# Receptance, second low-rank and gate weights split ahead into DRAM, partly beside the first stage

## The chip, the cores and the metric

One core of a Trainium2 chip runs the whole program. The metric is the device time of one execution in microseconds (us); the median of the runs stands for a kernel.

## The reference

Two residual layers over 512 tokens of width 1024, each followed by a gated convolutional FFN. Layer 0 mixes tokens with a chunked spatial gate, layer 1 is RWKV-7. All of it is float32.

```python
# layer 0
z = gelu(h @ w_in + b_in);  u, v = split(z);  v = rms_norm(v, g_v)
v = einsum(causal w_s, v in blocks of 128) + b_s
h = h + (u * v) @ w_out
# layer 1
xx = token_shift(h) - h;  xr, xw, xk, xv, xa, xg = (h + xx * mu[i] for i in range(6))
r = xr @ w_r;  k = xk @ w_k;  v = xv @ w_v
w = -softplus(-(w0 + tanh(xw @ w1) @ w2)) - 0.5
a = sigmoid(a0 + (xa @ a1) @ a2)
g = sigmoid(xg @ g1) @ g2
y = wkv7_scan(r, exp(-exp(w)), k, v, -kk, kk * a)      # a 64x64 state per head, 16 heads
h = h + (group_norm(y) * ln_w + ln_b + bonus) * g @ w_o
# after each layer
h = h + (silu(gate) * val) @ w_down,  gate, val = split(conv3(rms_norm(h) @ w_up) + conv_b)
```

## The kernel before

Activations lie transposed in SBUF, eight tiles `h[k]` of 128 features by 512 tokens. A float32 product is made of three matmuls in the faster 32-bit format (`mm3`, lines 295 to 297): a number x is split into a high part, ScalarE's cast of x (line 213, tiles named `wh`, `mxh` and so on), and a low part, x minus the high part, a subtraction on VectorE (line 214, `wl`, `mxl`; GpSimd does some of the activations' ones). The parts' products high·high, low·high and high·low add up in PSUM.

The stages follow each other on the one core: the spatial gate (`sgu`), the first FFN (`ffn`, 22 steps of two up-projections, then eight down-projections), RWKV, the second FFN, the final norm. In RWKV, `rwkv_first` makes the first low-rank products and the receptances r, and `rwkv_main` weaves three things: the chunk products and the scan, the inversion of small triangular blocks, and a filler of dense projections (keys, values, gates, output).

Weights come in tiles of 128 by 1024. `weights()` (line 229) loads a tile raw into one of two buffers `w32` and splits it, in halves of 512 columns, into `wh` and `wl`, four buffers of each. A raw tile is so loaded up to two tiles ahead, and the casts run up to four halves ahead of TensorE; a cast waits until TensorE is done with the buffer that it writes.

For keys, values, output and the first gate weights (`wk`, `wv`, `wo`, `g1`) the splitting has been done earlier. `make_parts()` (line 242) is a generator; each step loads one piece of 128 by 512 (`pw`, two buffers), casts it to `pwh`, subtracts to `pwl` (one buffer each) and stores both to DRAM (`wkd`, `wvd`, `wod`, `g1d`), all DMAs on SP's queue. The first FFN takes two steps of it per up-projection step for the first 15 of them, one for the rest, and two per down-projection. `parts()` (line 261) then loads the ready parts straight into `wh` and `wl`.

The receptances still use `weights()`. `wra` holds the first 512 output features as four tiles, each with two k: TensorE runs k = 0 to 7, four outputs each, three matmuls each, 96 in all; between, each k's operand is scaled (line 673), mixed (`mix`, lines 623 and 624) and split. `wrb` holds the other 512 as four tiles of one output each, taken in two pairs; in a pair TensorE goes over k and gives each of the two tiles three matmuls per k. The second low-rank factors (`second_factors`, lines 726 to 731) are loaded raw by SP four times, two pairs of features each, cast by ScalarE and subtracted by VectorE. The second gate weights (`gate_weights`, line 1063) are loaded on ScalarE's queue, 128 rows and 32 rows, the latter stacked (`stack`, line 219): high, high and low part in three groups of 32 rows.

What sets the order: each engine executes its instructions in the order written down by the framework's scheduler, which places an instruction of low priority where its model finds the engine free; `issue_after` ties a step behind the last instruction of an engine. DMAs stand in the queue of the engine that issues them (ScalarE or SP), and a DMA that waits for a buffer holds back everything behind it on that engine.

## Time and profile before

| | us |
|---|---|
| median of the 3 runs (1298.95, 1301.09, 1313.26) | 1301.09 |
| the profiled execution | 1305.46 |
| its span, first to last instruction | 1303.7 |
| TensorE busy / idle in the span | 1262.6 / 41.1 |
| VectorE, ScalarE, GpSimd busy | 852.5, 627.9, 129.9 |
| spatial gate, about | 0 to 155 |
| first FFN, about | 155 to 524 |
| `rwkv_first`, about | 524 to 582 |
| products and scan, about | 582 to 905 |
| second FFN and final norm, about | 905 to 1304 |

Rows of the profile name engines as PE (TensorE matmuls), PEld (TensorE weight loads), DVE (VectorE), ACT (ScalarE), POOL (GpSimd) and SP; ACTq and SPq are the issuing of DMAs in ScalarE's and SP's queues. L213 is line 213 of the kernel before. In a timeline a row is start, duration, engine, line, operation, output and inputs; in brackets the engine's idle time before it and what ended that. A matmul's shown length overlaps the next one's start, so its pace is read from start to start.

### The profile page before, as it was taken

The page shows a single profiled execution, that of the slowest core. Times are in us where ns is not written, and L with a number is a line of the kernel's source. Part 1 is how long each engine was busy: PE and PEld are TensorE (multiplying, and loading weights), DVE is VectorE, ACT ScalarE, POOL GpSimd, SP SyncE. Part 2 cuts the span into 40 slices and gives each one's busy share as a digit, 9 for nine tenths or more (in the row PEclk, how much of TensorE's full clock was granted, in tenths as well). Part 3 has the DMA queues.
Part 4 walks back from the last instruction along what each step waited for, and adds up shares of the span by engine and source line. Part 5 has one row for each costly group of instructions (what it writes and reads, how often), then busy time and mean ns, then how long its engine had stood idle before and what let it go on. Part 6 is the DMA issues. An engine that isn't in the chain of part 4 may idle for free.

```text
span 1303.7 us, 19609 instructions
## 1 busy us (share of the span) xinstructions
PE 1262.6 (97%) x7578; PEld 1015.2 (78%) x7578; DVE 852.5 (65%) x1379; ACT 627.9 (48%) x1072; POOL 129.9 (10%) x140
## 2 busy tenths in 40 slices
PE   8999999999999999999999988999999999999996
PEld 6878888888888888777777766767888888888886
DVE  5565478888875444756889686754677777772223
ACT  5544455555554333565776636512544444442221
POOL 3100100000000001210121011321200000000001
PEclk9999999999999999999999899999999999999998
DMA  7332458777557664336888697795233233333332
GB/s 254 96 102 83 130 177 249 246 247 241 172 170 218 202 214 154 89 112 164 242 225 264 171 239 177 179 223 156 82 99 98 97 97 98 97 95 102 89 89 77
DMA packets 110924, 205.84 MB, mean 158 GB/s; under 512 B 18224, under 2 KB 50224, under 8 KB 110832
## 3 DMA queue, kind: packets, MB, share of 16 engines
q10 hardware_dynamic: 39024, 113.66, 29.1%
q1 hardware_dynamic: 71808, 90.95, 24.0%
q8 instruction: 59, 0.97, 0.3%
q14 instruction: 33, 0.27, 0.1%
HBM read 155.02 MB, written 49.55 MB: 157 GB/s over the span
## 4 chain that ended last, share of the span: by engine, by line
PE 78%; DVE 8%; issue 3%; DMA 3%; ACT 2%; POOL 1%; SPq 0%; ACTq 0%; DVEq 0%; POOLq 0%
PE mm L295 8%; PE mm L297 8%; PE mm L296 8%; PE aux L295 6%; PE aux L296 6%; PE aux L297 6%; PE us L297 5%; PE us L295 5%; PE us L296 5%; PE e L297 5%; PE e L296 5%; PE e L295 5%; DVE pr L973 1%; DVE tt L974 1%; DVE lq L900 1%
## 5 line engine op out<-in xcount | busy, mean ns | idle before, releaser
L213 ACT CAST wh<-w 128x512 fp32r<-128x512 f32 x340 | 206.3, 610 | 344.9 <-PE mm L296 87.7
L214 DVE TENSOR_TENSOR wl<-w,wh 128x512 fp32r<-128x512 f32 x340 | 232.0, 684 | 179.7 <-ACT wh L213 178.2
L295 PE MATMUL mm<-mxh,wh 128*128 128x512 f32 (+1 forms) x384 | 156.9, 409 | 0.0
L297 PE MATMUL mm<-mxh,wl 128*128 128x512 f32 (+1 forms) x384 | 153.2, 399 | 0.3 <-DVE wl L214 0.3
L296 PE MATMUL mm<-mxl,wh 128*128 128x512 f32 (+1 forms) x384 | 152.1, 396 | 0.0
L322 POOL TENSOR_TENSOR ss<-ss,sq 128x512 f32<-128x512 f32 x30 | 40.9, 1364 | 783.9 <-issue 594.9
L519 ACT ACTIVATE cv<-z,par 128x512 f32<-128x512 f32 x88 | 71.7, 817 | 42.3 <-DVE z L517 42.2
L295 PEld LDWEIGHTS mm<-mxh,wh 128*128 128x128 f32 (+1 forms) x384 | 72.4, 188 | 18.0 <-issue 2.6
L297 PEld LDWEIGHTS mm<-mxh,wl 128*128 128x128 f32 (+1 forms) x384 | 72.4, 189 | 17.6 <-DVE wl L214 0.8
L295 PE MATMUL e<-mxh,wh 128*128 128x512 f32 x216 | 84.5, 391 | 0.0
L296 PEld LDWEIGHTS mm<-mxl,wh 128*128 128x128 f32 (+1 forms) x384 | 72.5, 189 | 15.4 <-issue 0.7
L296 PE MATMUL e<-mxl,wh 128*128 128x512 f32 x216 | 84.1, 389 | 0.0
L297 PE MATMUL e<-mxh,wl 128*128 128x512 f32 x216 | 84.1, 389 | 0.0
L296 PE MATMUL aux<-mxl,wh 128*128 128x512 f32 x208 | 81.4, 391 | 2.7 <-POOL mxl L214 2.0
L295 PE MATMUL aux<-mxh,wh 128*128 128x512 f32 x208 | 81.5, 392 | 0.3 <-ACT mxh L213 0.3
L295 PE MATMUL us<-mxh,wh 128*128 128x512 f32 x208 | 81.2, 391 | 0.0
L520 DVE SCALAR_TENSOR_TENSOR cv<-z,par,cv 128x512 f32<-128x512 f32 x88 | 66.1, 751 | 22.9 <-ACT cv L519 22.6
L297 PE MATMUL aux<-mxh,wl 128*128 128x512 f32 x208 | 81.0, 390 | 0.0
L297 PE MATMUL us<-mxh,wl 128*128 128x512 f32 x208 | 81.0, 389 | 0.0
L296 PE MATMUL us<-mxl,wh 128*128 128x512 f32 x208 | 80.9, 389 | 0.0
L521 DVE SCALAR_TENSOR_TENSOR cv<-z,par,cv 128x512 f32<-128x512 f32 x88 | 66.0, 752 | 2.9
L296 PEld LDWEIGHTS aux<-mxl,wh 128*128 128x128 f32 x208 | 39.1, 188 | 12.3 <-POOL mxl L214 2.7
(1091 smaller groups left out, 2700.3 us busy)
## 6 DMA issues: line engine op xcount, KB each, us to landing
w<-in_wup ACTq DMA_DIRECT2D x88, 512.0 KB, 3.7
w<-in_wdn ACTq DMA_DIRECT2D x32, 512.0 KB, 3.6
st<-std SPq DMA_DIRECT2D x30, 384.0 KB, 5.8
std<-lq SPq DMA_DIRECT2D x32, 256.0 KB, 4.4
w<-in_wdn ACTq DMA_DIRECT2D x16, 384.0 KB, 3.4
w<-in_wsu ACTq DMA_DIRECT2D x8, 512.0 KB, 3.6
w<-in_wso ACTq DMA_DIRECT2D x8, 512.0 KB, 3.6
pw<-in_wk SPq DMA_DIRECT2D x16, 256.0 KB, 3.8
```

The source lines that it names most:

```text
L213: nc.scalar.copy(hi[r, :n], src)
L214: (lo_eng or nc.vector).tensor_tensor(lo[r, :n], src, hi[r, :n].bitcast(F32), ALU.subtract)
L295: mm(acc, wh, xh, start=first, stop=False)
L296: mm(acc, wh, xl, start=False, stop=False)
L297: mm(acc, wl, xh, start=False, stop=last)
L322: nc.gpsimd.tensor_tensor(self.ss, self.ss, self.sq, ALU.add)
L519: nc.scalar.activation(c, z[:, 2:], AF.Identity, scale=cw(2, i), bias=self.p("conv_b", l * 44 + i))
L520: nc.vector.scalar_tensor_tensor(c, z[:, 1:T + 1], cw(1, i), c, ALU.mult, ALU.add)
L521: nc.vector.scalar_tensor_tensor(c, z[:, 0:T], cw(0, i), c, ALU.mult, ALU.add)
L900: V.tensor_tensor(lq[:, :, 1 - hd], qs[hd], masks.unsqueeze(1).to_broadcast([P, U, P]), ALU.mult)
L973: V.tensor_tensor(q, a, b, ALU.mult)
L974: V.tensor_tensor(tt[:, 0:nj, j + 1:32], tt[:, 0:nj, j + 1:32], q, ALU.add)
```

## The change

`make_parts` takes a list of pieces. The list (`part_list`) now also holds `wra` and `wrb` (16 pieces), the second low-rank factors `l2` (4) and the second gate weights `g2` (4): 75 pieces instead of 51. The first 21 (all of `wra` and `wrb`, five of `wk`) are made in the spatial gate: six beside its v products, ten beside u and the gating, six beside its output, with one step to drain. The other 54 are made in the first FFN, which takes two steps per up-projection step for 17 instead of 15 of them. The receptances load their parts with `parts()` on ScalarE's queue, eight halves of two DMAs for `wra` and as many for `wrb`; the second factors come as three DMAs on SP's queue instead of two, with no cast and no subtraction; the gate weights come on SP's queue instead of ScalarE's, without cast, subtraction or stacking.

```diff
@@ part_list and make_parts
+        for n, ds in self.wd.items():                  # wra, wrb, wk, wv, wo
+            for m, d in enumerate(ds):
+                for c in (slice(0, 512), slice(512, 1024)):
+                    at.append((A[n][m][:, c], [(j, rows, d[:, j, c]) for j in range(2)]))
...
-                    src, _, c = at[i]
-                    w.append(pool.tile([P, 512], F32, tag="pw", bufs=2, name=self.uid("pw"))[:, 0:c.stop - c.start])
-                    nc.sync.dma_start(w[i], src[:, c])
+                    src = at[i][0]
+                    r, n = src.shape
+                    w.append(pool.tile([P, 512], F32, tag="pw", bufs=2, name=self.uid("pw"))[0:r, 0:n])
+                    nc.sync.dma_start(w[i], src)
                 if i:
...
+                    if r == 32:
+                        x = [None, None, pool.tile([P, 512], F32R, tag="pwh", bufs=1, name=self.uid("pws"))]
+                        self.stack(x[2], w[i - 1], False)
+                    else:
+                        x = self.split(pool, w[i - 1], [P, 512], "pw", bufs=1)
+                    for j, rows, dst in at[i - 1][1]:
+                        nc.sync.dma_start(dst, x[j][rows, 0:n].bitcast(F32))
@@ sgu
+            parts = self.make_parts(sp, self.part_list()[:SGU_PARTS])
                     w = self.weights(A["wsv"][hf, kk], cut=hf == kk == 0)
+                    for _ in range((0, 0, 1, 1, 1, 1, 1, 1)[4 * hf + kk]):
+                        next(parts, None)
...
                 w = self.weights(A["wsu"][m])
+                if m < KT - 1:
+                    next(parts, None)
...
                 y.append(self.split(sp, t, [P, T], f"y{m}"))
+                if m % 2 == 0 and m < 6:
+                    next(parts, None)
...
                 w = self.weights(A["wso"][m])
+                if 0 < m < KT - 1:
+                    next(parts, None)
@@ ffn
-            parts = self.make_parts(fp) if self.next == "rwkv" else iter(())
+            parts = self.make_parts(fp, self.part_list()[SGU_PARTS:]) if self.next == "rwkv" else iter(())
-                for _ in range(2 if j < 15 else 1):
+                for _ in range(2 if j < 17 else 1):
@@ rwkv_first
-            w = self.weights(A["wra"][kk])
+            w = self.parts("wra", kk, False)
-            ws = [self.weights(A["wrb"][m + j]) for j in range(2)]
+            ws = [self.parts("wrb", m + j, False) for j in range(2)]
@@ second_factors
-            for j in range(2):
-                w = w32[:, 512 * j:512 * j + 2 * P]
-                nc.sync.dma_start(w, A["l2"][j][:, P * p:P * p + 2 * P])
-                S.copy(l2[j], w)
-                V.tensor_tensor(l2[2][H[j]], w[H[j]], l2[j][H[j]].bitcast(F32), ALU.subtract)
+            for i, t in enumerate(l2):
+                nc.sync.dma_start(t.bitcast(F32), self.l2d[:, i, P * p:P * p + 2 * P])
@@ gate_weights
-            self.wq.dma_start(w32[:, 0:512], A["g2"][0:P, cols])
-            self.wq.dma_start(w32[0:32, 512:], A["g2"][P:P + 32, cols])
-            ws = ep.tile([P, 512], F32R, tag="gw", bufs=1, name=self.uid("gw"))
-            self.stack(ws, w32[0:32, 512:], False)
-            return (*self.split(ep, w32[:, 0:512], [P, 512], "gw", bufs=1), ws)
+            t = [ep.tile([P, 512], F32R, tag=f"gw{i}", bufs=(2, 2, 1)[i], name=self.uid("gw")) for i in range(3)]
+            for i, n in enumerate((P, P, 96)):
+                nc.sync.dma_start(t[i][0:n].bitcast(F32), self.g2d[g][0:n, i])
+            return t
```

The order of the instructions moves with it, at three places above all (line numbers of the change differ from those of the kernel before; a tile's name is followed by running numbers).

First, VectorE at the start of the receptances, from the first scaling of h to the low part of the first operand `mxl` (`mt` is a mixed operand, `lt` and `lu` the scaled low-rank products). Before:

```order
L673 SCALAR_TENSOR_TENSOR h0_66<-h0_66,par_65,rb_917_4597 128x512
L673 SCALAR_TENSOR_TENSOR h1_67<-h1_67,par_65,rb_917_4597 128x512
L214 TENSOR_TENSOR wl_935_4676<-w32_933_4673,wh_934_4675 128x512
L624 SCALAR_TENSOR_TENSOR mt_927_4633<-h0_66,omu_4458,mt_927_4633 128x512
L624 SCALAR_TENSOR_TENSOR mt_930_4654<-h1_67,omu_4458,mt_930_4654 128x512
L673 SCALAR_TENSOR_TENSOR h2_68<-h2_68,par_65,rb_917_4597 128x512
L214 TENSOR_TENSOR mxl_929_4637<-mt_927_4633,mxh_928_4636 128x512
```

and in the change:

```order
L711 SCALAR_TENSOR_TENSOR h1_67<-h1_67,par_65,rb_987_4798 128x512
L711 SCALAR_TENSOR_TENSOR h2_68<-h2_68,par_65,rb_987_4798 128x512
L711 SCALAR_TENSOR_TENSOR h3_69<-h3_69,par_65,rb_987_4798 128x512
L662 SCALAR_TENSOR_TENSOR mt_996_4832<-h0_66,omu_4659,mt_996_4832 128x512
L662 SCALAR_TENSOR_TENSOR mt_999_4853<-h1_67,omu_4659,mt_999_4853 128x512
L693 TENSOR_TENSOR lt_1012_4922<-aux_981_4748,rb_987_4798 128x512
L694 TENSOR_TENSOR lu_1013_4923<-e_982_4749,rb_987_4798 128x512
L218 TENSOR_TENSOR mxl_998_4836<-mt_996_4832,mxh_997_4835 128x512
```

The weight's subtraction is gone; the low part of the first operand stands behind four scalings of h (the first one is the row ahead of these) and both low-rank products instead of three scalings and a subtraction.

Second, ScalarE at the same place, from the copy of the norm `rb` to the cast of the first operand `mxh`. Before:

```order
L340 COPY rb_917_4597<-mm_916_4592 128x512
L213 CAST wh_934_4675<-w32_933_4673 128x512
L623 ACTIVATE mt_927_4633<-h0_66,par_65 128x512
L623 ACTIVATE mt_930_4654<-h1_67,par_65 128x512
L213 CAST mxh_928_4636<-mt_927_4633 128x512
L213 CAST wh_936_4679<-w32_933_4673 128x512
```

and in the change:

```order
L369 COPY rb_987_4798<-mm_986_4793 128x512
L301 DMA wh_1002_4872<-wrad1_103 128x512
L661 ACTIVATE mt_996_4832<-h0_66,par_65 128x512
L661 ACTIVATE mt_999_4853<-h1_67,par_65 128x512
L301 DMA wl_1003_4873<-wrad1_103 128x512
L301 DMA wh_1004_4876<-wrad1_103 128x512
L217 CAST mxh_997_4835<-mt_996_4832 128x512
```

The second tile's cast and its raw tile are replaced by four loads; that of its second half (`wh_1004`), which takes the last buffer of the second low-rank product, stands now ahead of the first operand's cast and not behind it.

Third, ScalarE where the first pair of `wrb`'s tiles ends and the second begins (`rt` takes the finished receptances). Before:

```order
L693 COPY rt1_4523<-aux_978_4864 128x512
L213 CAST wh_986_4928<-w32_985_4926 128x512
L693 COPY rt1_4523<-e_979_4865 128x512
L213 CAST wh_988_4932<-w32_985_4926 128x512
L266 DMA w32_1036_5117<-wkd2_104 128x1024
```

and in the change:

```order
L301 DMA wh_1048_5113<-wrbd3_109 128x512
L731 COPY rt1_4724<-aux_1042_5053 128x512
L731 COPY rt1_4724<-e_1043_5054 128x512
L301 DMA wl_1049_5114<-wrbd3_109 128x512
L301 DMA wh_1050_5117<-wrbd3_109 128x512
L301 DMA wl_1051_5118<-wrbd3_109 128x512
```

Where the fourth tile was cast from a raw tile already in SBUF, its four loads are issued, three of them behind both copies.

34 lines of the change are left out of this document (23 added, 11 removed).

## Prediction

> **What bounds the kernel now.** I read the page first, then the table of stretches, then the list of what TensorE waited for, and last the timeline at the places that the change touches. The page names the engine:
>
> ```profile
> span 1303.7 us, 19609 instructions
> ...
> PE 1262.6 (97%) x7578; PEld 1015.2 (78%) x7578; DVE 852.5 (65%) x1379; ACT 627.9 (48%) x1072; POOL 129.9 (10%) x140
> ...
> PE 78%; DVE 8%; issue 3%; DMA 3%; ACT 2%; POOL 1%; SPq 0%; ACTq 0%; DVEq 0%; POOLq 0%
> ```
>
> TensorE is busy in all but 41.1 us. The change removes no matmul, so it can win only idle time, or time in which TensorE ran slow. Where the idle time lies, the stretches say (start:end, length, then busy us and count of each engine, granted clock, DMA share, GB/s):
>
> ```profile
> 0.00:50.00 50.00, 43.55 (x187) 35.52 (x188) 26.23 (x37) 27.21 (x49) 15.71 (x24) 1.00 0.64 218
> 50.00:100.00 50.00, 49.51 (x274) 39.35 (x274) 32.03 (x47) 21.80 (x40) 1.01 (x1) 1.00 0.27 85
> 250.00:300.00 50.00, 50.00 (x223) 41.38 (x222) 42.89 (x66) 29.87 (x49) 0.00 (x0) 1.00 0.77 243
> 530.00:560.00 30.00, 26.94 (x113) 20.27 (x112) 27.07 (x35) 19.39 (x33) 8.28 (x6) 1.00 0.29 86
> 600.00:720.00 120.00, 116.31 (x909) 89.45 (x910) 100.67 (x185) 80.58 (x157) 19.25 (x19) 1.00 0.82 235
> 720.00:900.00 180.00, 163.65 (x2186) 121.19 (x2185) 118.27 (x256) 80.56 (x160) 36.26 (x40) 0.95 0.77 193
> 1050.00:1100.00 50.00, 50.00 (x223) 41.40 (x222) 37.48 (x55) 24.58 (x38) 0.00 (x0) 1.00 0.29 95
> 1250.00:1303.70 53.70, 42.65 (x256) 37.46 (x254) 16.87 (x30) 11.48 (x22) 7.76 (x8) 0.91 0.26 82
> ```
>
> Start and end hold 6.5 and 11.1 us, which the change doesn't touch. Within reach are 3.1 us at the receptances (530 to 560), 3.7 in the products (600 to 720), 16.4 in the scan (720 to 900). In 530 to 560 VectorE is full: 27.1 of 30 us. That is where splits are taken away.
>
> **The change part by part.** *The added splitting.* 21 pieces move beside the first stage, 3 more go into the first FFN (54 pieces against 51). A piece costs ScalarE and VectorE one instruction each and SP three DMAs:
>
> ```profile
> L214 DVE TENSOR_TENSOR pwl<-pw,pwh 128x512 fp32r<-128x512 f32 (+1 forms) x51 | 34.8, 683 | 15.2 <-DMA wkd<-pwl 5.0 <-DMA wvd<-pwl 4.5 <-ACT pwh L213 1.8
> L213 ACT CAST pwh<-pw 128x512 fp32r<-128x512 f32 (+1 forms) x51 | 31.3, 614 | 9.4 <-DMA wkd<-pwh 4.2 <-DMA wvd<-pwh 2.7 <-DMA wod<-pwh 1.5
> L731 DVE TENSOR_TENSOR l<-w,l 64x256 fp32r<-64x256 f32 x8 | 3.3, 418 | 5.5 <-ACT l L730 5.4
> L730 ACT CAST l<-w 128x256 fp32r<-128x256 f32 x8 | 3.1, 404 | 6.8 <-DMA w<-in_l 6.7
> ```
>
> So the first stage gets 14.3 us of VectorE and 12.9 us of ScalarE. About 8 pieces fall into 50 us there: VectorE goes from 32.0 to 37.5. The first FFN carries 42.9 with its pieces, and its TensorE issues 223 matmuls in 50 us, just as many as the second FFN's 223 without pieces. So splitting beside dense matmuls costs nothing on average, and the cover is the two weight tiles by which the casts run ahead of TensorE. It gets thin at one place, the normalization of v:
>
> ```profile
> 60.56 4.87 DVE L443 SCALAR_TENSOR_TENSOR vt<-vt,rv,bvg 128x1024 f32<-128x1024 f32 x4 [1.12 <-POOL rv L348]
> ...
> 66.69 0.50 PE L297 MATMUL mm<-mxh,wl 128*128 128x512 f32 x1 [0.33 <-DVE wl L214]
> ```
>
> VectorE is shut there for 4.9 us and TensorE already waits 0.33 us. One more piece stands behind the first split: I take +0.3 us. Bounds: 0, and +3.0 if ScalarE, whose next piece waits for the last one's store, blocks once for a whole landing (2.8 us, below).
>
> *The receptances, what goes.* The first half of them (wra, four tiles of weights, two k each) is 96 matmuls:
>
> ```profile
> 530.54 1.42 DVE L673 SCALAR_TENSOR_TENSOR h<-h,par,rb 128x512 f32<-128x512 f32 x2 [1.75 <-ACT rb L340]
> ...
> 533.25 0.62 ACT L213 CAST mxh<-mt 128x512 fp32r<-128x512 f32 x1 [0.31 <-DVE mt L624]
> ...
> 533.61 0.39 PE L297 MATMUL e<-mxh,wl 128*128 128x512 f32 x1
> ...
> 533.93 0.50 PE L295 MATMUL aux<-mxh,wh 128*128 128x512 f32 x1
> ...
> 535.20 0.50 PE L296 MATMUL aux<-mxl,wh 128*128 128x512 f32 x1
> ...
> 557.72 0.39 PE L295 MATMUL aux<-mxh,wh 128*128 128x512 f32 x1
> 560.44 0.39 PE L295 MATMUL aux<-mxh,wh 128*128 128x512 f32 x1
> ```
>
> Twelve undisturbed matmuls take 2.72 us (557.72 to 560.44), so 96 need 21.8; they took 26.5 (533.93 to 560.44). 4.7 us are lost to operands that come late, because VectorE does per k a scaling, a mix, the low parts and a weight split. After the change the weight splits are gone. By the order shown above the first operand is later, not earlier: ScalarE casts it only behind a load that waits for the end of the second low-rank product (about 533.84), so at 534.0 to 534.6, and VectorE makes its low part behind four scalings, two mixes and two more products, eight steps of about 0.65 us from 530.54: 535.7 to 536.4. TensorE loses 0.7 and then 0.95 us. From the second operand on I find both engines ahead of it. 4.7 - 1.65 gives 3.0 us gained by the end of the 96.
>
> *The receptances, what comes.* Before, a weight lay raw in SBUF and only a cast and a subtraction stood between the free buffer and its use. Now a load does, issued in ScalarE's queue:
>
> ```profile
> w<-in_wrb ACTq DMA_DIRECT2D x4, 512.0 KB, 3.7
> ...
> wkd<-pwh SPq DMA_DIRECT2D x16, 256.0 KB, 2.8
> ```
>
> ```profile
> L272 ACTq DMA_DIRECT2D wh<-wkd x12: 326/354/1145, 576.6 to 633.7; - x12
> ...
> DMA to landing us min/median/max: 3.2/4.5/6.8
> ```
>
> Within wra a half tile is freed three halves (8.2 us) ahead, which covers a landing. It doesn't at two places, both where a pair of wrb's tiles begins. In the first pair the second tile's first half gets a buffer about 2.8 us before the 96 end and is needed three matmuls (0.7 us) after: lead 3.5. In the second pair the high part of the same half goes out 1.1 us before the first pair's end and is needed 8 matmuls (1.8 us) after: lead 2.9; its low part stands behind two copies, but TensorE has 16 matmuls before it. With a landing of 4.0 us (between 3.7 for the loads at this place and 4.5 for the same kind of load where the DMA share is higher) TensorE waits 0.5 + 1.1 = 1.6. Net of the stage: -1.4 us. Bounds: -3.0 with 3.2, and +6.5 with 6.8 (3.3 + 3.9, and 2.3 at wra's third tile, whose load ScalarE issues behind the low-rank casts, 4.5 us ahead: 9.5, less 3.0).
>
> The Trainium skill, page "DMA: Bandwidth & Descriptors", section "Anatomy of one DMA", fits 2.0 us plus bytes at 436 GB/s per DMA (for GpSimd's path); as an estimate 2.6 us for 256 KB, at which neither place would wait and the sum would be 1.6 us lower. The trace does not agree: no load of this size on ScalarE's queue landed under 3.2 us.
>
> *The second factors and the gate.* The list of TensorE's waits has both:
>
> ```profile
> PE mm L805 <- ACT vt L796: 2.3, 3, 1.8
> ...
> PE aux L296 <- POOL mxl L214: 2.0, 2, 1.2
> ...
> PE e L821 <- ACT l L730: 1.7, 2, 1.0
> ```
>
> The second factors' splits go; their parts come by SP, which holds three DMAs of 128 KB where it held two, and needs no shared raw buffer. I take -1.5 of the 1.7 us, bounds -1.7 and +1.0 (a reload behind a store of SP's queue). The gate's first split is the costlier one:
>
> ```profile
> 753.43 0.75 ACT L1159 COPY y<-e 64x256 f32<-64x256 f32 x2 [0.55 <-PE e L1156]
> 758.62 0.62 ACT L213 CAST gwh<-w 128x512 fp32r<-128x512 f32 x1 [4.44 <-DMA w<-in_g]
> ...
> 759.26 0.74 ACT L796 COPY vt<-mm 64x256 f32<-64x256 f32 x2
> ...
> 760.82 1.12 PE L805 MATMUL mm<-rt,wb 128*128 128x512 f32 x2 [1.77 <-ACT vt L796]
> ...
> 764.22 0.63 PE L297 MATMUL mm<-mxh,wl 128*128 128x512 f32 x1
> 764.65 0.63 PE L295 MATMUL mm<-mxh,wh 128*128 128x512 f32 x1
> ```
>
> ScalarE stands 4.44 us at the cast, which waits for the load; the copies of vt behind it come late, and TensorE waits 1.77 us for them. After the change no cast stands there. I take -1.8; bounds 0 (the copies find another wait) and -3.0 (matmuls after the stall start 0.43 us apart, not 0.23; some 1.2 us more).
>
> *The new order of the products and scan.* The same work stands otherwise on all queues. I take 0; bounds two waits of 1.8 us (the longest here) gained or lost, 3.6 either way.
>
> **Sum:** +0.3 - 1.4 - 1.5 - 1.8 = -4.4 us. The profiled execution took 1305.5 us (span 1303.7 and 1.8 around it), 4.4 above the median of the runs; that gives 1301.1 for it, and 1296.7 against the median of 1301.1.
>
> **The rivals.** *Late loads (slower).* The receptances' weights arrive 6.8 us after issue, and the three places cost 9.5 us against 3.0 gained. It decides from a landing of about 4.7 us on (there the stage's net is 0). For it: 4.5 is the median of such loads. Against: a DMA share of 0.29 here, 0.82 there; the stage doubles its 4 MB, to perhaps 0.5. Time: 1301.1 + 6.5 + 0.3 - 1.5 - 1.8 = 1304.6.
>
> *A faster scan.* From 720 to 900 the granted clock averages 0.95, 9 us worth of full speed. If a ScalarE and VectorE freed of gate splits keep TensorE fed, half may come back: 1292.2. Against: most stalls there are the scan's own chain. The Trainium skill, page "TensorE: Matmul & The Clock Gate", section "Part 1: The HAM clock gate", says that an idle window of about 3.4 us halves the clock; the slow matmuls after 760.82 agree, though that stall is only 1.77 us.
>
> *No gain.* The waits named are only the last of several: what the stage and the gate give back, the next late thing takes. For it: the new order puts the first operand later. Time: 1301.1.
>
> **How the numbers follow.** Forecast 0.5, late loads 0.2, no gain 0.13, faster scan 0.12, none of these 0.05. A measurement of this kernel tells about 1% (13 us) from no change; all cases lie inside that. Faster by over 1% needs nearly all gains at their bounds (0.06), slower needs late loads and a bad order together (0.04); within 1%, 0.90. The range goes from 1289 (the lower bounds of stage, factors, gate and order, -3.0 - 1.7 - 3.0 - 3.6 = -11.3, rounded down) to 1307 (late loads and two thirds of the order's bound).
>
> **What would show it.** Right: the 96 matmuls take about 23.4 us, TensorE waits for DMAs of wh at the starts of both pairs for about 0.5 and 1.1 us, the first stage's idle time grows by under 1 us, the waits at l and behind gwh are gone. Wrong: waits for wh of 2 us and more at the receptances, over 2 us of new idle time before 150 us, or a granted clock in the scan over 0.97.

## The result and the profile after

The change made the kernel slower. Its median is 1315.7 us (1310.0 to 1320.6, 10 runs) against 1305.0 for the kernel before in the same runs: ratio 1.0061, 95% interval 1.0041 to 1.0082. Timed again later (12 runs) the ratio was 1.0042 (1.0022 to 1.0062). So it costs between 5 and 8 us where 4.4 us of gain were forecast; 1315.7 lies outside the predicted range, which ended at 1307. "Within 1%" holds. The profiled execution took 1314.6 us. Its page begins so, and its fourth part so (line numbers of the change: up to 34 higher than before; L217 is the cast, L218 the subtraction, L324 to L326 are `mm3`, L242 the load in `weights`, L286 the store of a piece, L475 the normalization of v, L503 the gating product):

```profile
span 1312.5 us, 19811 instructions
...
PE 1265.8 (96%) x7578; PEld 1018.0 (78%) x7578; DVE 850.8 (65%) x1375; ACT 626.2 (48%) x1068; POOL 130.7 (10%) x140
...
PE 77%; DVE 9%; issue 3%; DMA 2%; ACT 2%; POOL 1%; ACTq 0%; DVEq 0%; SPq 0%; POOLq 0%
```

The span grew by 8.8 us; 5.6 of them are new idle time of TensorE (41.1 to 46.7), the other 3.2 are busy time in as many matmuls, which took longer: the clock granted over the span fell from 0.989 to 0.984. The table of stretches (those of before, moved by 6 us from the receptances on):

```profile
0.00:50.00 50.00, 43.57 (x188) 35.53 (x189) 29.48 (x42) 30.10 (x54) 15.89 (x24) 1.00 0.84 278
50.00:100.00 50.00, 47.17 (x256) 36.76 (x255) 31.55 (x48) 21.76 (x42) 1.01 (x1) 0.97 0.65 202
100.00:150.00 50.00, 49.04 (x243) 38.62 (x242) 34.69 (x52) 25.66 (x44) 6.30 (x4) 1.00 0.74 227
...
536.00:566.00 30.00, 27.92 (x115) 22.33 (x114) 19.11 (x24) 14.00 (x24) 7.00 (x6) 0.94 0.58 175
606.00:728.00 122.00, 118.19 (x882) 91.52 (x880) 96.20 (x172) 76.88 (x147) 19.50 (x19) 0.94 0.82 230
728.00:906.00 178.00, 160.62 (x2204) 119.02 (x2200) 115.93 (x250) 78.70 (x155) 36.40 (x40) 0.96 0.80 199
```

Look at 50 to 100 us: TensorE was busy 49.5 of 50 us there and is now 47.2, VectorE no busier than before (31.6 against 32.0), and the share of the DMA engines went from 0.27 to 0.65. At the receptances VectorE fell as forecast, from 27.1 to 19.1 of 30 us.

To see where time is lost I read five starts off TensorE's timeline in every profile: the sum-of-squares product of each norm (L359), and the first and last score product (L930). Between them lie the first stage, the first FFN, the low-rank products with receptances, the products, and the scan with the output. In us, one profiled execution each:

| kernel | first stage | first FFN | receptances | products | scan, output | ratio to before (95%) |
|---|---|---|---|---|---|---|
| before | 129.1 | 362.6 | 84.8 | 129.9 | 190.9 | |
| before_again | 129.0 | 362.6 | 85.2 | 132.7 | 193.0 | |
| the change | 135.1 | 362.6 | 85.1 | 133.4 | 190.7 | 1.0061 (1.0041 to 1.0082) |
| after_again | 133.7 | 362.6 | 84.8 | 131.4 | 194.6 | 1.0042 (1.0022 to 1.0062) |
| sgu_only | 134.9 | 362.6 | 84.9 | 133.0 | 189.9 | 1.0035 (1.0007 to 1.0063) |
| sgu_bufs2 | 132.9 | 362.6 | 85.0 | 132.7 | 193.4 | 1.0030 (1.0005 to 1.0055) |
| sgu_deep | 132.4 | 362.6 | 85.1 | 129.9 | 190.3 | 1.0030 (1.0001 to 1.0059) |
| sgu_after_norm | 136.5 | 362.6 | 84.8 | 131.9 | 190.7 | 1.0058 (1.0033 to 1.0082) |
| sgu_dma_only | 140.9 | 362.6 | 85.3 | 130.3 | 194.2 | 1.0076 (1.0050 to 1.0103) |
| sgu_cast_only | 129.1 | 362.6 | 84.9 | 130.1 | 193.4 | 0.9997 (0.9977 to 1.0017) |
| ffn0_all | 129.1 | 408.4 | 85.1 | 132.2 | 192.4 | 1.0386 (1.0344 to 1.0429) |
| ffn0_all_deep | 129.0 | 370.6 | 85.2 | 135.1 | 194.2 | 1.0076 (1.0046 to 1.0105) |
| recept_only | 129.0 | 385.3 | 85.6 | 133.0 | 190.9 | 1.0176 (1.0127 to 1.0225) |
| recept_wso | 129.0 | 362.6 | 85.3 | 134.4 | 190.1 | 0.9995 (0.9972 to 1.0017) |
| small_only | 129.0 | 362.6 | 85.0 | 131.5 | 190.9 | 0.9989 (0.9963 to 1.0014) |
| wra_only | 129.0 | 362.6 | 84.6 | 134.0 | 192.3 | 1.0001 (0.9981 to 1.0022) |
| wrb_only | 129.0 | 362.6 | 84.6 | 130.0 | 186.5 | 0.9991 (0.9964 to 1.0017) |
| wrb_small_wso | 129.0 | 362.6 | 85.5 | 135.1 | 190.1 | 1.0017 (0.9995 to 1.0038) |

The first two columns repeat to 0.1 us wherever a stage is undisturbed; the last two vary by several us between two executions of one kernel (before and before_again: 2.8 and 2.1). So the first stage's 6.0 us (4.6 in the second profile) belong to the change, and the 3.5 of the products can't be told from spread: over all eighteen profiles the products took 129.9 to 135.1 us with the small weights (second factors and gate) stored (eleven kernels, mean 132.1) and 129.9 to 134.4 without (seven, mean 132.4).

**Inside the first stage.** ScalarE's timeline of the change, as v's second half comes to its end:

```profile
47.53 0.62 ACT L217 CAST pwh<-pw 128x512 fp32r<-128x512 f32 x1 [2.92 <-DMA wrad<-pwh]
...
48.28 0.55 ACTq L242 DMA_DIRECT2D w<-in_wsu  x1
...
52.00 0.62 ACT L217 CAST pwh<-pw 128x512 fp32r<-128x512 f32 x1 [1.95 <-DMA wrad<-pwh]
...
54.73 0.62 ACT L217 CAST wh<-w 128x512 fp32r<-128x512 f32 x1 [2.11 <-DMA w<-in_wsu]
56.78 0.63 ACT L468 ACTIVATE vt<-vt 128x512 f32<-128x512 f32 x1 [1.43 <-DVE vt L466]
```

A piece's cast stands 2.92 us at the head of the queue until the store of the piece before it has landed. The load of `wsu` behind it goes out at 48.28 (45.52 before), its cast waits 2.11 us for it, and the activations of v begin at 56.78 instead of 53.77.

The last row names a second wait. The activations need VectorE's step on v (L466, L434 before), and VectorE stands in order at the same piece's low part. Its step before, then in the change, and the store that the low part waited for, with its time to landing:

```profile
52.98 0.75 DVE L434 SCALAR_TENSOR_TENSOR vt<-e,rt,bvg 128x512 f32<-128x512 f32 x1 [2.06 <-PE e L297]
```

```profile
55.39 0.69 DVE L218 TENSOR_TENSOR pwl<-pw,pwh 128x512 fp32r<-128x512 f32 x1 [4.39 <-ACT wh L217]
56.00 0.74 DVE L466 SCALAR_TENSOR_TENSOR vt<-e,rt,bvg 128x512 f32<-128x512 f32 x1
```

```profile
49.83 0.32 SPq L286 DMA_DIRECT2D wrad<-pwl  x1
...
DMA to landing us min/median/max: 5.5/5.5/5.5
```

The profile puts VectorE's 4.39 us down to ScalarE's cast of `wh`, which ended last before it, at 55.35; but the subtraction reads nothing of that cast. In the instruction list VectorE waits from 50.10 to 55.35 on two DMA semaphores: that of the piece's load, which had landed at 49.52, and that of this store, which landed at 55.31 and set the one buffer of `pwl` free. So two waits, ScalarE's for its weight and VectorE's for a piece's store, end within 0.1 us of each other, and taking away one leaves the other.

The normalization of v follows (63.59 against 60.56), and then TensorE:

```profile
64.93 0.44 PE L503 MATMUL aux<-ws,vt 128*64 128x128 f32 x4 [0.56 <-DVE vt L475]
66.13 0.44 PE L503 MATMUL aux<-ws,vt 128*64 128x128 f32 x4 [0.76 <-DVE vt L475]
67.32 0.44 PE L503 MATMUL aux<-ws,vt 128*64 128x128 f32 x4 [0.76 <-DVE vt L475]
68.52 0.60 PE L503 MATMUL aux<-ws,vt 128*64 128x128 f32 x4 [0.76 <-DVE vt L475]
...
70.74 0.63 PE L325 MATMUL mm<-mxl,wh 128*128 128x512 f32 x1
71.16 0.63 PE L326 MATMUL mm<-mxh,wl 128*128 128x512 f32 x1
```

It takes the four blocks of v one by one as they come, 2.8 us of waits, and the matmuls after that stand 0.42 us apart instead of 0.23 for about 3 us. The second gating product starts 4.1 us later than before (78.50 against 74.44). The rest is lost ahead of the first gating product (0.6 us in this profile, none in the second) and at y6 and y7, whose casts and subtractions stand behind pieces':

```profile
118.75 0.50 PE L325 MATMUL us<-y6l,wh 128*128 128x512 f32 x1 [0.21 <-DVE y6l L218]
...
120.01 0.49 PE L324 MATMUL us<-y7h,wh 128*128 128x512 f32 x1 [0.52 <-ACT y7h L217]
```

From y7's end on, beside the output product, nothing more is lost (44.8 us to the first FFN, before and now). So the stage has three places. Their times, from the first norm to the first gating product, from there to the second, and from the last gating product to the second output product:

| | to first gating | v: first to second gating | y: last gating to second output |
|---|---|---|---|
| before | 33.2 | 10.0 | 6.7 |
| the change, after_again | 33.9, 33.2 | 13.6, 13.6 | 8.4, 7.7 |
| sgu_bufs2, sgu_deep | 33.2, 33.2 | 13.8, 13.3 | 6.7, 6.7 |
| sgu_after_norm | 33.2 | 10.0 | 13.9 |
| sgu_cast_only, recept_wso | 33.2, 33.2 | 10.0, 10.0 | 6.7, 6.7 |

### The profile page after: what moved, and what is told of

It reads as the page before. It is cut to its first block, busy times and chain, and to the rows that moved or that the text cites. A ratio compares the mean times of both kernels' runs of the same rounds, so it can differ in the third digit from the quotient of the medians.

```text
span 1312.5 us, 19811 instructions
## 1 busy us (share of the span) xinstructions
PE 1265.8 (96%) x7578; PEld 1018.0 (78%) x7578; DVE 850.8 (65%) x1375; ACT 626.2 (48%) x1068; POOL 130.7 (10%) x140
## 4 chain that ended last, share of the span: by engine, by line
PE 77%; DVE 9%; issue 3%; DMA 2%; ACT 2%; POOL 1%; ACTq 0%; DVEq 0%; SPq 0%; POOLq 0%
PE mm L324 8%; PE mm L326 8%; PE mm L325 8%; PE aux L324 6%; PE aux L325 6%; PE aux L326 6%; PE us L326 5%; PE us L325 5%; PE us L324 5%; PE e L324 5%; PE e L326 5%; PE e L325 5%; DVE pr L1007 1%; DVE tt L1008 1%; POOL gr L377 1%
## 5 line engine op out<-in xcount | busy, mean ns | idle before, releaser
L217 ACT CAST wh<-w 128x512 fp32r<-128x512 f32 x324 | 196.0, 610 | 311.4 <-PE mm L325 76.8
L218 DVE TENSOR_TENSOR wl<-w,wh 128x512 fp32r<-128x512 f32 x324 | 224.2, 695 | 156.9 <-ACT wh L217 156.2
L324 PE MATMUL mm<-mxh,wh 128*128 128x512 f32 (+1 forms) x384 | 156.7, 408 | 1.5 <-DMA wh<-wrbd 0.7
L326 PE MATMUL mm<-mxh,wl 128*128 128x512 f32 (+1 forms) x384 | 152.4, 397 | 0.0
L324 PEld LDWEIGHTS mm<-mxh,wh 128*128 128x128 f32 (+1 forms) x384 | 72.2, 188 | 20.2 <-issue 3.7
L326 PEld LDWEIGHTS mm<-mxh,wl 128*128 128x128 f32 (+1 forms) x384 | 72.4, 188 | 16.5 <-DVE wl L218 0.4
L324 PE MATMUL e<-mxh,wh 128*128 128x512 f32 x216 | 84.9, 393 | 0.0
L326 PE MATMUL e<-mxh,wl 128*128 128x512 f32 x216 | 84.4, 391 | 0.0
L324 PE MATMUL aux<-mxh,wh 128*128 128x512 f32 x208 | 81.4, 391 | 0.8 <-ACT mxh L217 0.8
L324 PE MATMUL us<-mxh,wh 128*128 128x512 f32 x208 | 81.2, 391 | 0.0
L326 PE MATMUL aux<-mxh,wl 128*128 128x512 f32 x208 | 81.2, 390 | 0.0
L326 PE MATMUL us<-mxh,wl 128*128 128x512 f32 x208 | 81.2, 390 | 0.0
L218 DVE TENSOR_TENSOR pwl<-pw,pwh 128x512 fp32r<-128x512 f32 (+1 forms) x73 | 51.1, 700 | 36.9 <-ACT wh L217 11.4
```

Source lines behind the costliest of these rows:

```text
L217: nc.scalar.copy(hi[r, :n], src)
L218: (lo_eng or nc.vector).tensor_tensor(lo[r, :n], src, hi[r, :n].bitcast(F32), ALU.subtract)
L324: mm(acc, wh, xh, start=first, stop=False)
L326: mm(acc, wl, xh, start=False, stop=last)
```

## The experiments

Each kernel was timed beside the kernel before, and "above before" goes by the ratio of the two; before_again is a profile alone.

### Which part of the change costs: ffn0_all, sgu_only, recept_only, small_only

ffn0_all makes all pieces in the first FFN:

```diff
-SGU_PARTS = 21
+SGU_PARTS = 0
...
-            parts = self.make_parts(sp, self.part_list()[:SGU_PARTS])
+            parts = iter(())
...
-                for _ in range(2 if j < 17 else 1):
+                for _ in range(3 if j < 16 else 2):
```

> All 75 pieces are split beside the first FFN (3 steps in each of its first 16 iterations, 2 in the rest), none beside the first stage; the receptances, the factors and the gate read the stored parts as in the change. Theory FIRST STAGE (the profile of the change has its first FFN begin 5.8 us later than before; ScalarE and VectorE, which take their work in order, stand behind the pieces' casts and late weight loads there): the 5.8 us go, first FFN begins at 160.3 us again, and the time is about 1310 (1307 to 1311), that is 4 to 6 us above the kernel before at most. Rival RWKV STAGE (the stored parts are read late and stall TensorE there): the time stays near the change's 1316, 10 above before. Rival FULL VECTORE IN THE FFN (75 pieces fill it from 42.9 to about 46 of 50 us): the first FFN, 362.6 us long before and in the change, becomes 3 us longer or more.

Measured 1357.4 us, 50 above before. The first stage was as before, as the theory said, but the first FFN took 408.4 us. No theory had that: of the rival with the full VectorE the direction came true, but VectorE was busy 32.2 of 50 us. In the profile of this kernel a stretch of the FFN, then who waited for the pieces' stores (L286) between 160 and 560 us (us, times), then ScalarE's timeline over one FFN iteration:

```profile
250.00:300.00 50.00, 40.81 (x156) 29.78 (x155) 32.22 (x50) 23.19 (x38) 0.00 (x0) 0.95 0.73 227
```

```profile
  ACT pwh L217: 87.2, 43
  DVE pwl L218: 22.0, 21
```

```profile
241.59 0.62 ACT L217 CAST hid5h<-cv 128x512 fp32r<-128x512 f32 x1
...
251.57 0.62 ACT L217 CAST pwh<-pw 128x512 fp32r<-128x512 f32 x1 [4.34 <-DMA wkd<-pwh]
...
256.24 0.62 ACT L217 CAST hid6h<-cv 128x512 fp32r<-128x512 f32 x1 [0.31 <-DVE cv L562]
```

ScalarE stood 87 us at `pwh`, 43 times, for a store's landing. In the kernel before two such casts, six iterations apart, are (the list of L213's instructions between 160 and 520 us; start of first and last)

```profile
L213 ACT CAST hid0h<-cv x1: 617/617/617, 176.1 to 176.1; 128x512 fp32r<-128x512 f32 x1
...
L213 ACT CAST hid6h<-cv x1: 621/621/621, 239.1 to 239.1; 128x512 fp32r<-128x512 f32 x1
```

so an iteration takes about 10.5 us there (63.0 over six) and 14.7 here. (The 16.2 us that my expectations give for an iteration are wrong.) That makes a new theory, ROUND TRIP. With one buffer for `pwh`, a piece's cast can begin only when the last one has been cast (0.62 us) and its store has landed. The issue lists of the first FFN, before and in ffn0_all, have for it (median us to landing in the last column; 2.5 to 3.2 for the other large weights before, 3.4 to 4.0 in ffn0_all)

```profile
wvd<-pwh SPq DMA_DIRECT2D x16, 256.0 KB, 2.9
```

```profile
wkd<-pwh SPq DMA_DIRECT2D x16, 256.0 KB, 4.0
wvd<-pwh SPq DMA_DIRECT2D x16, 256.0 KB, 4.0
```

so a chain of 3.1 to 3.8 us a piece before and of 4.0 to 4.6 in ffn0_all, whatever the engines have free. Two fit into 10.5 us (7.6 at most), three of ffn0_all's (12.1 to 13.9) don't, and since the cast stands in ScalarE's in-order queue, everything behind it comes late.

sgu_only splits as the change does and puts the three readers back to `weights()`, `second_factors` and `gate_weights` of before:

```diff
-            w = self.parts("wra", kk, False)
+            w = self.weights(A["wra"][kk])
...
-            ws = [self.parts("wrb", m + j, False) for j in range(2)]
+            ws = [self.weights(A["wrb"][m + j]) for j in range(2)]
...
```

> The splitting is as in the change, 21 pieces beside the first stage and 54 in the first FFN, but the receptances, the second factors and the gate load and split their own weights as before, so the 24 new pieces are stored for nobody: the price of the splitting alone. Theory FIRST STAGE: first FFN begins 5.8 us later than before, at about 166, and the time is 5 to 7 us above the kernel before (about 1311). Rival RWKV STAGE: no more than 2 us above before, since the loss comes with the reading.

Measured 1312.0, 4.6 us above before (0.9 to 8.2), with the first FFN beginning at 166.2: the splitting alone costs what the change costs. TensorE's instructions stand in the order of before (24 of 7578, which start within 0.4 us of each other, change places), and yet its products took 133.0 us. So the kernel before was profiled again (below).

recept_only (all in the first FFN, 3 steps in its first 8 iterations, `l2` and `g2` as before):

> Only the receptances' weights (16 pieces) are added to the stored parts, all of them in the first FFN (67 pieces); the second factors and the gate stay as before. Theory FIRST STAGE: from the last matmul of the first FFN to the end of the receptances' first 96 matmuls 0.6 us less than before, and the time within 3 us of before (1302 to 1307). Rival RWKV STAGE: 3 us or more above before, with TensorE waiting for the loads of wh at the receptances and slower clocks behind.

Measured 1330.1. Again the first FFN, not the reading: 22.7 us more for 8 iterations of three pieces, 2.8 each; ffn0_all's 45.8 for 16 are 2.9 each. That the loss goes with the count of such iterations fits ROUND TRIP.

small_only (all in the first FFN, `range(2)`, `wra` and `wrb` as before):

> Only the second factors and the gate's weights (8 pieces) are added to the stored parts, in the first FFN (59 pieces); the receptances split their own weights as before. Theory FIRST STAGE: no wait for l and for the gate's vt (3.5 us of waits fewer), the time 0 to 3 us below before (1302 to 1305). Rival RWKV STAGE: the three-part loads on SP land late, or the order that follows makes TensorE wait for sq and for ti elsewhere, and the time is 2 us or more above before.

Measured 1306.7, ratio 0.9989: 59 pieces at two an iteration cost the FFN nothing. The waits at l and at the gate's vt are gone as expected, but a wait of 3.3 us at sq stands in the products.

### Where in the first stage, and by what: sgu_bufs2, sgu_after_norm, sgu_deep, sgu_dma_only, sgu_cast_only

sgu_bufs2 gives the parts two buffers, in the first stage only (the first FFN has no room):

```diff
-            parts = self.make_parts(sp, self.part_list()[:SGU_PARTS])
+            parts = self.make_parts(sp, self.part_list()[:SGU_PARTS], bufs=2)
...
-                        x = self.split(pool, w[i - 1], [P, 512], "pw", bufs=1)
+                        x = self.split(pool, w[i - 1], [P, 512], "pw", bufs=bufs)
```

> The change with one edit: beside the first stage the two parts of a piece have two buffers each in place of one, so that a cast needn't wait for the landing of the store just before it. Traffic, instructions and their places stay. Theory ROUND TRIP (ScalarE, in order, stands at pwh until the last store has landed, and what is queued behind it, weight casts, weight loads and the activations of v, comes late): the 2.9 and 1.95 us waits of pwh for a store between 43 and 53 us go, w<-in_wsu is issued on time, v's normalization begins near 61 us in place of 63.6 and the first FFN 3 to 5 us sooner than in the change (161 to 163 us); time about 1311. Rival TRAFFIC (the pieces' transfers make the weight loads land 2 to 3 us later, 5.5 us in place of 3.6): waits stay at w<-in_wsu, the first FFN begins at 165 or later, and the time stays at the change's 1316.

Measured 132.9 us for the stage, 2.2 less than the change in its first profile and 0.8 less than in its second. The 1.7 us at y went, the 3.6 at v did not: ScalarE stood there for a piece's load (2.0 us) and for w<-in_wsu (4.4 us) in place of the stores. VectorE's step on v was back in its place (21.75 us after the first norm's product, as before; 24.92 in the change), and v's activations were late all the same, behind ScalarE's 4.4 us. So ROUND TRIP is right for y; at v it is right for VectorE's wait, and TRAFFIC for ScalarE's, which alone is enough for the loss.

sgu_after_norm casts no piece before v is normalized (`SGU_PARTS = 15`, no step beside v's products nor with the first value; 60 pieces in the first FFN):

> The change with its pieces moved: none is cast before v is normalized (none in v's second half, none with the first value), 15 in the rest of the first stage, 60 in the first FFN at 2 steps an iteration; one buffer a part as in the change. Theory ROUND TRIP: the 4.1 us that the change lost between 65 and 78 us go, the 1.7 us at y6 and y7 stay; first FFN begins at about 162, and the time is about 1311 to 1312. Rival VECTORE (its load, not the wait, makes the value steps late): the second gating product still comes 2 us or more later than the 74.4 us of before.

The second gating product came 10.0 us after the first, as before, so VECTORE fell and what was lost at v was gone. But the stage took 136.5 us: TensorE then waited 4.8 us at y6. There are three pieces to two value steps of about 6.7 us, 4.5 us a piece. The nine casts of `pwh` beside the value steps came 5.1 us apart (73.77 to 114.60), and in the change 5.3 (72.63 to 115.37); so y6 was cast 87.1 us after the first norm's product, in the change 86.3, though the second gating product came 4.2 us sooner here. What the change loses at v hides most of what its pieces cost at y. The forecast of 1.7 us for that place failed.

sgu_deep adds four buffers for the loaded piece, asked for three steps ahead (`bufs=2, ahead=3`):

> The change with deeper buffers beside the first stage: two buffers for each part and four for the loaded piece, which is asked for three steps ahead in place of one, so that ScalarE waits neither for a store's landing nor for a piece's load. Theory WAITS (what is lost there is ScalarE standing in order at pwh for the piece's own transfers): from the first norm's matmul to the first FFN's 129 to 131 us (129.1 before, 135.1 in the change, 132.9 with two buffers for the parts alone). Rival TRAFFIC (the pieces' transfers make the loads of wsu land at 6 us in place of 3.6): 132 us or more, with ScalarE waiting for w<-in_wsu before v's activations.

Measured 132.4, and v again 3.3 us late: ScalarE hardly waits for pieces any more (1.3 us), but for the stage's own weights. The first rows are ScalarE's waits between 36 and 165 us in the change, the second those of sgu_deep (us in total, times, longest):

```profile
ACT pwh L217 <- DMA wrad<-pwh: 5.6, 3, 2.9
...
ACT pwh L217 <- DMA wrbd<-pwh: 4.8, 3, 2.4
ACT wh L217 <- DMA w<-in_wsu: 4.1, 3, 2.1
```

```profile
ACT wh L217 <- DMA w<-in_wsu: 8.7, 3, 5.0
```

The 10.4 us at `pwh` are gone and the 4.1 at w<-in_wsu have become 8.7. By the expectation's own mark (132 or more) the remainder is TRAFFIC. The first such load in sgu_deep, from issue to the cast that waited for it, took 7.3 us; before, it was issued 0.4 us sooner after the norm's product and landed in 3.6:

```profile
41.84 0.34 ACTq L242 DMA_DIRECT2D w<-in_wsu  x1
...
49.17 0.62 ACT L217 CAST wh<-w 128x512 fp32r<-128x512 f32 x1 [5.01 <-DMA w<-in_wsu]
```

The issue lists between 36 and 165 us (KB each, median us to landing) of before, the change and sgu_deep:

```profile
w<-in_wsu ACTq DMA_DIRECT2D x8, 512.0 KB, 3.6
```

```profile
w<-in_wsu ACTq DMA_DIRECT2D x8, 512.0 KB, 5.5
```

```profile
w<-in_wsu ACTq DMA_DIRECT2D x8, 512.0 KB, 5.4
```

And 42 to 56 us of the same three (the two last columns are DMA share and GB/s):

```profile
42.00:56.00 14.00, 14.00 (x68) 11.74 (x67) 5.79 (x9) 5.32 (x10) 0.00 (x0) 1.00 0.50 146
```

```profile
42.00:56.00 14.00, 14.00 (x67) 11.76 (x66) 4.87 (x8) 4.54 (x8) 0.00 (x0) 1.00 0.83 277
```

```profile
42.00:56.00 14.00, 14.00 (x68) 11.71 (x67) 7.69 (x12) 4.74 (x10) 0.00 (x0) 1.00 0.97 313
```

The DMA engines go from half to 0.83 and, where nothing holds the pieces back, 0.97 busy, and a 512 KB load takes 1.8 to 1.9 us longer at the median. The pieces go by SP's queue and the weights by ScalarE's. The Trainium skill, page "DMA: Bandwidth & Descriptors", section "Issuing engines are not separate DMA queues", says that transfers run on the same 16 engines and interleave, whichever engine started them; these rows agree.

sgu_dma_only keeps the transfers and leaves out cast and subtraction:

```diff
+                    elif cut:
+                        x = self.split(pool, w[i - 1], [P, 512], "pw", bufs=1)
                     else:
-                        x = self.split(pool, w[i - 1], [P, 512], "pw", bufs=1)
+                        x = (w[i - 1].bitcast(F32R),) * 2
...
```

> The change without the splitting of the 21 pieces beside the first stage: they are loaded and stored as they are, the same bytes on the same queue, with no cast and no subtraction (so the receptances read whole weights in the place of both parts, which takes as long). Theory WAITS: no engine stands at a piece, and the first FFN begins 129 to 130.5 us after the first norm. Rival TRAFFIC: the loads of wsu land late all the same, and it is 132 us or more.

Measured 140.9 us for the stage, the longest of all, so not WAITS as expected; but as a test of TRAFFIC it failed too, since other waits came in. ScalarE's waits in this kernel:

```profile
ACT wh L217 <- DMA w<-in_wsv: 7.4, 1, 7.4
...
ACT u L493 <- DMA wrbd<-pw: 6.5, 1, 6.5
```

The load of `wsv` stood behind pieces in SP's queue, and u's activation, which has nothing to do with a piece, ended its wait with a piece's store: ahead of it in the queue a load of wsu waited to be issued, in the instruction list on a DMA semaphore which that store used as well: the store landed at 82.87, the load went out at 82.97. I read from it only that the stage is slow without any splitting. In the change no such wait stands ahead of v's activations: the loads of wsu at 48.28 and 52.03 take semaphores whose last transfers had landed at 47.44 and 49.52. Elsewhere in the stage such waits weren't tried apart from the transfers' landing.

sgu_cast_only does the opposite, on the base of small_only: at the 21 places a tile in SBUF is split, with no transfer.

```diff
+            raw = sp.tile([P, 512], F32, name="raw")
+            nc.gpsimd.memset(raw, 1.0)
...
+                    self.split(sp, raw, [P, 512], "pw", bufs=1)
```

> The kernel with only the small weights stored (first stage 129.0 us from the first norm to the first FFN, 0.1% below before), and beside its first stage, at the change's 21 places, the cast and the subtraction of a tile of ones that is already there: the engines' work of the 21 pieces without their loads and stores. What these splits make is used by nothing. Theory TRANSFERS (the loss is waits for pieces' transfers and late weight loads): the first stage takes 129 to 130 us. Rival ENGINE WORK (14 us of VectorE and 13 of ScalarE crowd the value steps): 132 us or more.

Measured 129.1 us for the stage and 1306.4 in all, as before. ENGINE WORK falls: 14 us of VectorE and 13 of ScalarE cost nothing there. The loss comes with the pieces' transfers.

### Three pieces an iteration with deeper buffers: ffn0_all_deep

```diff
-                        x = self.split(pool, w[i - 1], [P, 512], "pw", bufs=1)
+                        x = self.split_in_place(pool, w[i - 1])
...
-    c = fp.tile([P, T], F32, tag="cv", bufs=4, name=self.uid("cv"))
+    c = fp.tile([P, T], F32, tag="cv", bufs=3, name=self.uid("cv"))
```

> All 75 pieces in the first FFN at 3 steps an iteration, as in the run that took 1357 us, but with deeper buffers: the low part is written over the loaded piece, three such pieces in place of two, and two high parts in place of one; the room comes from the conv's tiles, three in place of four. Theory ROUND TRIP (one piece's cast, store and landing take 5 to 6 us, three don't fit into the 16.2 us of an iteration with one buffer, and ScalarE stands at pwh meanwhile): the first FFN falls from 408.4 us to 362.6 to 370, and the time to 1306 to 1316. Rival LOAD (VectorE, ScalarE or the transfers of three pieces are too much for an iteration): the first FFN stays above 390 us.

Measured 370.6 us for the FFN, against 408.4 with the same pieces and one buffer: 37.8 of the 45.8 us went with the buffers (370.6 is 0.6 over the expected band, and 1319.7 us in all 3.7 over it). The high part, the low part and the loaded piece got deeper buffers together, so the share of each isn't known. Left are 8.0 us, in stretches like this one with VectorE at 44.3 of 50 us and a DMA share of 0.95; which of the two takes them wasn't tried.

```profile
250.00:300.00 50.00, 49.09 (x212) 39.45 (x213) 44.31 (x68) 30.67 (x50) 0.00 (x0) 1.00 0.95 294
```

### Place or number: recept_wso

`SGU_PARTS = 6`, all steps beside the output product, `range(2)` in the first FFN and two steps more in its down-projections, `l2` and `g2` as before:

> Only the receptances' weights are added (67 pieces), as in the run that took 1330 us; but 6 pieces lie in the last third of the first stage, beside the output product, where the change's own pieces cost nothing (y7 to the first FFN 44.8 us before and in the change), and 61 in the first FFN at 2 steps an iteration. Theory PLACE (dense matmuls with one piece to 5.6 us or two to 16.2 are free, the value steps and three to an iteration are not): first stage 129.0 us, first FFN 362.6, and the time as before within 3 us. Rival NUMBER (the 67 pieces cost wherever they lie): 5 us or more above before.

Measured 1307.8, ratio 0.9995; recept_only with the same 67 pieces took 1330.1. PLACE holds: where TensorE has 5.2 us and more of its own per piece, the splitting cost nothing that can be told.

### What the reading gives: wra_only, wrb_only, wrb_small_wso

On the base of recept_only with `range(2)`, only one of the two weights is stored.

> Only wra (8 pieces) is added to the stored parts, in the first FFN at 2 steps an iteration, which 59 pieces fill as in the run with the small weights alone (0.1% below before, its interval to both sides). So the price of reading wra is seen without the price of splitting it. By the prediction on record: 1.3 us gained and no stall (1303 to 1305). By the profile of the change, in which TensorE took 25.0 us for the 96 matmuls in place of 26.5 but began them 0.9 us later and waited for mxl 1.2 us at a lower clock: nothing won or lost, within 2 us of before. Rival RWKV STAGE: 3 us or more above before.

> Only wrb (8 pieces) is added to the stored parts, in the first FFN at 2 steps an iteration. Its loads wait, in ScalarE's queue, for the ring of weight tiles, and the second pair's come late: in the change TensorE stood 0.7 us at wh<-wrbd. By the prediction on record: 1.6 us lost (0.5 at the first pair, 1.1 at the second). By the profile of the change: about 1 us lost, within 2 us of before. Rival RWKV STAGE: 3 us or more above before, through the order of the products behind it.

Measured 1307.7 (ratio 1.0001) and 1305.6 (0.9991): neither costs nor gains anything that can be told. wrb_small_wso stores `wrb`, `l2` and `g2`, with the placing of recept_wso:

> wrb, the second factors and the gate's weights are read from stored parts, wra is split at its place as before; 67 pieces, 6 of them beside the output product of the first stage and 61 in the first FFN at 2 steps an iteration. Theory PLACE: first stage 129.0 us and first FFN 362.6, so the splitting is free, and the time is that of before less what the reading gives: 0 to 3 us below before (wrb alone 0.09% and the small weights alone 0.11% below, each uncertain by 0.25%). By the prediction on record the factors and the gate give 3.3 us and wrb loses 1.6: 1.7 below. Rival READING: 2 us or more above before.

Measured 1309.8, 1.0017 (0.9995 to 1.0038), that is 2.2 us above before, from 0.7 below to 5.0 above. The forecast of 1.7 us of gain lies outside. None of these kernels beats the kernel before.

### Spread: before_again, after_again

> The kernel before, unedited, profiled a second time. In its first profile the products (first to last score product, L896) took 129.9 us and what lies between the last product and the second FFN's norm 190.9; in the run with only the splitting, whose TensorE order is that of before row for row, the products took 133.0. Theory SPREAD: one kernel's products and scan differ by 3 us from one execution to the next, so the 3.5 us that the change lost there don't belong to it: here the products take 131 to 134 or the rest of the stage differs by 2 us or more. Rival READING (the stored parts make the products late): the products take 129.9 again within 0.5, and only kernels with other work beside them differ.

> The change, unedited, profiled and timed again. Theory SPREAD: the first stage takes 135 us again, the products between 130 and 134 us and the rest of the stage to the second FFN between 186 and 195 independently of it, and the time is 6 to 8 us above before. Rival ORDER (the change's order of the products costs 3 us): the products take 133 us or more and the time is 9 us or more above before.

before_again took 132.7 us for the products, where the first profile had 129.9: SPREAD holds. after_again was 5.5 us above before, with 133.7 for the first stage and 131.4 for the products: ORDER falls. The spans of the two second profiles, 1311.9 and 1307.3, differ by 4.6 us, and the first stage by 4.6 (133.67 against 129.04).

## Why the prediction was wrong

**The added splitting (+0.3, measured +6.0 and +4.6): the step that failed.** The engine work was costed, and rightly at nothing (sgu_cast_only). What was left out is the transfers. The mechanism stood in the bounds, "whose next piece waits for the last one's store", but priced as one landing of 2.8 us; it happened six times, for 10.4 us, at the head of ScalarE's queue, and at the head of VectorE's as well. It cost 1.7 us at y (1.0 in the second profile). The comparison with the first FFN ("223 matmuls in 50 us, just as many") took the mean of a stage that has 5.3 us for a piece (10.5 us, two pieces) for one that has 4.5, and the line between them is the chain of up to 4.6 us. A quantity per 50 us cannot show that; the piece's own chain, cast, store, landing, does. The larger part, 3.6 us at v, was left out altogether: what the pieces' transfers of 256 KB, three to a piece, do to the landing of `wsu`, just when ScalarE needs it ahead of v's activations (with VectorE's wait taken away, sgu_bufs2 and sgu_deep still lost 3.8 and 3.3 there).

Of the 12.4 us between the forecast and the result (9.9 by the second timing) this term is 5.7 (4.3). The three gains below, which did not show, are 4.7, and the rest lies within what the products and the scan differ by from one profile to the next.

**The receptances (-1.4, measured about 0).** The waits were the right ones; their sizes were off, and a slow stretch was left out. TensorE's rows in the change:

```profile
540.67 0.50 PE L324 MATMUL aux<-mxh,wh 128*128 128x512 f32 x1 [0.85 <-ACT mxh L217]
...
543.10 0.80 PE L325 MATMUL aux<-mxl,wh 128*128 128x512 f32 x1 [1.24 <-DVE mxl L218]
...
565.70 0.39 PE L324 MATMUL aux<-mxh,wh 128*128 128x512 f32 x1
...
579.66 0.47 PE L324 MATMUL mm<-mxh,wh 128*128 128x512 f32 x1 [0.71 <-DMA wh<-wrbd]
```

The 96 matmuls took 25.0 us (540.67 to 565.70), and began 0.9 us later relative to the norm, which the forecast had as 0.7. The forecast's 23.4 counts those 0.7 us, which lie ahead of the first matmul: by its own sum the 96 alone were to take 22.8. So 0.6 us were won by their end, not 3.0. The low part was late by 1.24 us (0.95 forecast), and after it the matmuls stood 0.43 us apart up to 546.3; this slow stretch, 1.7 us or so, was not in the sum. The wait at the second pair was 0.71 us (1.1 forecast); at the first pair there was none of note (0.5 forecast). The stage as a whole took 84.6 to 85.6 us in every profile, 84.8 and 85.2 before. (The prediction also says that no load of 256 KB on ScalarE's queue landed under 3.2 us. In the same profile five landed after 2.85 to 3.14 us; the figure is that of the loads of wkd that it shows.)

**Factors and gate (-1.5 and -1.8, measured none).** The waits at l and behind `gwh` are gone from the list. What came in their place, in the change between 520 and 950 us:

```profile
PE e L879 <- ACT sq L869: 3.8, 3, 1.7
...
PE aux L1028 <- DVE ix L1013: 2.6, 1, 2.6
```

In before and before_again these two were 1.5 and 1.6 to 1.7, with 1.5 to 1.7 at l and 2.3 to 2.4 at vt. That is no accident of one execution: in the eleven profiles with stored small weights sq is 3.3 to 4.2 and ix 2.4 to 2.6, in the seven without (before twice, sgu_only, wra_only, wrb_only, recept_only, recept_wso) 1.0 to 2.2 and 1.6 to 1.7. Some 4 us of waits went and some 3 came. This is the rival "no gain": the wait named was only the last of several. Why sq and ix come later was not tried. By its time, small_only alone would still allow the forecast's 3.3 us (its interval reaches 4.8 below); wrb_small_wso does not.

**The order of products and scan (0, bounds 3.6 either way).** +3.5 and -0.2 in the first profiles, but the kernel before differs from itself by 2.8 and 2.1.

**Rivals and signs.** Late loads was the one on the right side, for a wrong reason: the loads that came late were the first stage's, not the receptances'. Of the signs named for "wrong", the waits for wh of 2 us and more did not come (0.71), the new idle time before 150 us did: 3.3 us between 50 and 150 (2.34 and 0.96). The scan's clock stayed under 0.97 (0.96).

## What to carry to other kernels

Work that is put beside a busy stage has to be costed as a chain, from buffer to free buffer with its store's landing in it, and that chain compared with the time between two of them at the very place, not with the stage's mean. If a step of it stands in an in-order queue, its wait is the wait of all that is queued behind. Where the profile names an engine for a wait though the instruction reads nothing of what that engine made, look for a buffer that a store still holds. And before adding transfers, look at the share of the DMA engines there and at what loads the stage itself is about to need.

## What the runs showed of the hardware that was not expected

- The stores of the large weights' high parts (256 KB to DRAM, SP's queue) landed after 2.5 to 3.2 us at the median, by tensor, in the first FFN with two pieces an iteration and after 3.4 to 4.0 with three. Why is not shown: the share of the DMA engines hardly rose (0.71 and 0.74 between 165 and 365 us).
- The eight 512 KB loads of `wsu` took 3.6 us at the median with a DMA share of 0.33 between 36 and 165 us (before) and 5.5 with 0.66 (the change).
- Four waits of under 0.8 us within 4 us, or one of 0.85 and one of 1.24 within 3, were followed by matmuls at half pace (0.42 to 0.43 us apart instead of 0.23) for about 3 us.
- One kernel's products took 129.9 and 132.7 us, with nothing changed; its first stage and first FFN, of dense matmuls in the main, repeated within 0.1 us.
